# A decoder layer on eight cores: the last residual added by accumulating stores, norm stores moved to the GpSimd queue, and the first statistics interleaved with the K and V matmuls

## Chip, cores and metric

The kernel runs on one Trainium2 chip, as one program on all 8 cores (two dies of four). Each core computes 1024 of the 8192 tokens and reads all weights. The metric is the device time of the slowest core, in microseconds (us). Some executions of these kernels are in a second, slower state: the cores of one die show a lower granted TensorE clock and take longer (in one run of before, beside e1, cores 4 to 7 had a mean clock of 0.84 and took 7813 to 7819 us, cores 0 to 3 had 0.99 and took 6753 to 6769).

## The reference, cut

```python
# one layer, x is (1, 8192, 4096)
h = rms_norm(x, norm_mix_pre);  z = h @ w_in          # q, k, v, pool-in, two gates
y_attn = sliding_window_attention(q, k, v, sinks) @ w_branch_attn
y_pool = multiscale_pool(u, w_pool, pool_scale) @ w_branch_pool
merged = sigmoid(g_attn) * y_attn + sigmoid(g_pool) * y_pool
x = x + rms_norm(merged @ w_out, norm_mix_post)       # "x1": first residual norm
h = rms_norm(x, norm_ffn_pre)
up = causal_depthwise_conv(h @ w_up);  gate, val = split(up)
x = x + rms_norm((gelu(gate) * val) @ w_down, norm_ffn_post)      # "x2": second one
ple_gate = sigmoid(rms_norm(x, norm_ple_gate) @ w_ple_gate)
x = x + rms_norm(ple_gate * (p @ w_ple), norm_ple_post)           # last one, the output
```

A residual norm needs the sum of squares over all 4096 channels before it can scale the first of them. So its work comes in a burst, after the last matmul of one stage and beside the matmuls of the next.

## The kernel before

Features lie on partitions: D = 4096 is 32 chunks of 128, and a chunk of half the tokens is a 128x512 float32 tile of 256 KB. A scheduler records every operation of the program in order with its waits, and then each engine plays its own list. Every record comes from one helper, so all instructions carry one line number, L143 before and L144 after; they are told apart by their tiles.

Weights stream through a ring of 12 slots, each with a 256 KB slab of 8 blocks of 128x128. All weight loads are issued by GpSimd:

```python
def load_next(self):                       # cut
    i = self.nload % NS                    # NS = 12
    self.O("pool", "dma_start", [cast] if cast else [], [self.wringB[i]], dma=f"wr{i}",
           out=self.wring[i][:, 0:nk * 128], in_=src)

for kk in range(nk):                       # the matmuls of one slab, in run_jobs, cut
    self.O("pe", "matmul", [self.wringB[i]] + rb, [self.psB[bk]], ...)
    if side: ...self.side.popleft()()      # every `side` groups: one step of a norm
self.load_next()                           # then the load of the NEXT slab
```

In the program's order a load is only one slab ahead of the matmuls that use it. It runs farther ahead on the chip because GpSimd plays its list ahead of TensorE: a load waits only until TensorE has freed its slot (55 times and 95.1 us in the 130 us of before shown below), which allows up to 12 slabs, 96 groups of matmuls (a group is the matmuls with one 128x128 block).

The steps of a residual norm are put between the matmuls of the next stage by the `side` queue; each item taken from it is called a turn. Before, one step does everything for one chunk, and its store is on the Sync queue ("sp"):

```python
def main(k):                               # in norm_steps
    m, x, r = src[k], S["x"][k % NR], S["r"]
    O("dve", "tensor_tensor", [m.b, r.b], [m.b], out=m.v[:, 0:n], ..., op=ALU.mult)
    O("dve", "scalar_tensor_tensor", [m.b, x.b, constB], [m.b], ...)   # x gain, + residual
    ld_(k + NR)                            # residual chunk k+4, Sync queue
    put(k, m)                              # the store
    ...                                    # two ScalarE ops: square, and h in bf16
def put(k, m):                             # second norm
    O("sp", "dma_start", [m.b], [x2B[hf][k]], dma=f"x2s{k % 8}", out=x2_d[k][:, t0:t0 + 512], in_=m.v)
```

The last norm reloads x2 and adds it. Half 0 runs beside the matmuls of the per-layer-embedding stage (PLE, here also "last norm"); half 1 is the tail, after the last matmul:

```python
for f in range(NCH):                       # tail, cut
    m, x = R3[1][f], X2[f]                 # X2: x2 chunks loaded earlier
    O("dve", "tensor_tensor", [m.b, r.b], [m.b], out=m.v, in0=m.v, in1=r.v, op=ALU.mult)
    O("dve", "scalar_tensor_tensor", [m.b, x.b, constB], [m.b], ...)
    O("sp", "dma_start", [m.b], [outB], partial=True, dma="out", out=out_d[f][:, 512:1024], in_=m.v)
```

All those stores name one buffer, `outB`. The scheduler makes a writer wait for the buffer's earlier writers, with `partial=True` too:

```python
for b in writes:                           # Sched.op
    for d in (b.w, b.r):
        for k, v in d.items():
            if deps.get(k, 0) < v:
                deps[k] = v                # so each "out" store waits for the one before to land
```

The softmax here doesn't subtract the row's maximum and nothing guards it: scores larger than these inputs give would overflow.

## Time and profile before

| | before |
|---|---|
| times, us | 6766.01, 6785.48 (fast), 7415.28 (slow) |
| profiled span of the cores, us | 6735.2 to 6810.2 |
| TensorE idle, 0 to 560 us, core 6 | 93.7 |
| TensorE idle, 2200 to 3000 us (first norm), core 6 | 23.8 |
| TensorE idle, 5860 us to the last matmul (second norm and PLE), core 6 | 9.3 |
| last matmul to the end, core 6 | 78.3 |

The stage rows, here and later, are read from windows of 10 us: the part of each without TensorE busy, added up. "Lost to the clock" below is the busy time times one minus the granted clock of the window. I use core 6 for stages, because in the profiled execution of before cores 0 and 1 ran at a clock of 0.81 for much of the first 350 us (all of 200 to 340 us), and all four cores of their die at the end (0.81 from 6600 to 6680 us), while core 6's die was undisturbed (a mean clock of 0.990 to 0.991). Whole windows before that of the last matmul are counted, so up to 4 us of idle just before it are left out.

Lines of the page of the profile of before, slowest core (1): the span, busy time by engine, TensorE busy and its granted clock in 40 slices of the span in tenths, and the chain that ended last by engine.

```profile
span 6810.2 us, 104494 instructions; the slowest of 8 cores (6735.2 to 6810.2 us)
...
PE 6608.3 (97%) x41282; PEld 4044.9 (59%) x41282; DVE 1983.1 (29%) x2553; ACT 826.6 (12%) x1244; POOL 1335.0 (20%) x2501
...
PE   5999999999999998999999999999999999999995
...
PEclk7899999999999999999999999999999999999996
...
PE 92%; DMA 4%; DVE 2%; ACT 1%; issue 1%; POOL 0%; DVEq 0%; SPq 0%; ACTq 0%; POOLq 0%
```

TensorE is the bottleneck nearly everywhere: only the first and the last of the 40 slices, and a little the 16th (the first norm), are less than 90% busy. What a change elsewhere can win is therefore small, and what it can lose is not: TensorE has little idle time left in which a wait could hide (9.3 us on core 6 from 5860 us to the last matmul).

The chain that ended last, core 6 of before, from 0 to 200 us (start us, duration us, what):

```profile
22.04 47.36 DMA sb_arena<-w_in
...
73.61 17.50 DMA sb_arena<-xs
...
114.52 5.03 DMA sb_arena<-xs
...
144.46 5.70 DMA sb_arena<-xs
...
174.67 16.11 PE ps L143 x105
```

Each x slab holds up the chain again, since its statistics come after the K and V matmuls of the slab before. The streamed weights begin to be used near 175 us.

The waits of core 6 of before, 2580 to 2710 us, where the second half of the first norm runs (engine and tile, what it waited for, us in total, times, longest):

```profile
POOL sb_wr L143 <- PE ps L143: 95.1, 55, 5.9
...
DVE sb_arena L143 <- DMA sb_arena<-xr: 26.0, 14, 5.1
```

VectorE waits for the residual x, loaded by the Sync queue.

The tile `out` in the tail of core 6 of before (count, duration ns min/median/max, first and last start; then landing times):

```profile
L143 SPq DMA_DIRECT2D out<-sb_arena x32: 332/332/338, 6689.0 to 6760.1; - x32
...
DMA to landing us min/median/max: 2.0/2.1/2.7
```

32 stores take 71.1 us from first to last issue, (6760.1 - 6689.0)/31 = 2.29 us each, about the landing of one: this is the chain of stores through `outB`.

### The profile page before, as it was taken

What the parts mean: (1) busy time and instruction counts of PE and PEld (TensorE: products, weight loads), DVE (VectorE), ACT (ScalarE), POOL (GpSimd) and SP (SyncE); (2) the same over time, 40 slices, a digit from 0 to 9 for tenths busy, and PEclk for the clock granted to TensorE, in tenths of its full rate; (3) what the DMA queues carried; (4) which work ended last, traced back from release to release, by engine and by line L of the source; (5) the groups of instructions that cost most, each with busy time, mean ns of one, the idle gap of its engine ahead of it and who ended that gap; (6) DMA issues with size and microseconds to landing.
All of it is one profiled execution on the core that took longest, in us unless ns stands there. A gap on an engine that the chain in (4) does not pass through costs nothing.

```text
span 6810.2 us, 104494 instructions; the slowest of 8 cores (6735.2 to 6810.2 us)
## 1 busy us (share of the span) xinstructions
PE 6608.3 (97%) x41282; PEld 4044.9 (59%) x41282; DVE 1983.1 (29%) x2553; ACT 826.6 (12%) x1244; POOL 1335.0 (20%) x2501
## 2 busy tenths in 40 slices
PE   5999999999999998999999999999999999999995
PEld 3666666666665585766644566665456666444442
DVE  3343311111111125433300133331113333234343
ACT  2451000000001233000000000000000000023210
POOL 1011111111112322211111111111111111333331
PEclk7899999999999999999999999999999999999996
DMA  7457888888786577777799954446764444589683
GB/s 168 66 80 97 119 114 113 117 123 117 115 116 165 169 216 224 135 109 112 113 148 162 150 89 76 76 76 136 158 128 76 76 76 76 171 260 265 186 253 121
DMA packets 377375, 910.65 MB, mean 134 GB/s; under 512 B 50176, under 2 KB 72960, under 8 KB 371328
## 3 DMA queue, kind: packets, MB, share of 16 engines
q0 software_dynamic: 289344, 705.33, 60.3%
q1 hardware_dynamic: 87552, 198.64, 8.9%
q8 instruction: 337, 5.52, 0.3%
q14 instruction: 142, 1.16, 0.1%
HBM read 1297.47 MB, written 200.32 MB: 220 GB/s over the span
## 4 chain that ended last, share of the span: by engine, by line
PE 92%; DMA 4%; DVE 2%; ACT 1%; issue 1%; POOL 0%; DVEq 0%; SPq 0%; ACTq 0%; POOLq 0%
PE ps L143 92%; DVE sb_arena L143 2%; DMA out<-sb_arena 2%; DMA sb_arena<-xr 1%; ACT sb_arena L143 1%; DMA sb_arena<-w_in 1%; DMA sb_arena<-xs 0%; POOL sb_arena L143 0%; DMA sb_arena<-x_s 0%; DVEq L142 0%; ACT L143 0%; SPq L143 0%; ACTq L142 0%; SPq L142 0%; POOLq L168 0%
## 5 line engine op out<-in xcount | busy, mean ns | idle before, releaser
L143 PE MATMUL ps<-sb_arena,sb_wr 128*128 128x512 bf16 (+5 forms) x39744 | 6435.9, 324 | 20.1 <-DVE sb_arena L143 17.0
L143 PEld LDWEIGHTS ps<-sb_arena,sb_wr 128*128 128x128 bf16 x39744 | 3895.1, 98 | 2463.1 <-issue 112.6
L143 DVE TENSOR_TENSOR sb_arena<-ps,sb_arena 128x512 f32<-128x512 f32 (+9 forms) x892 | 682.2, 765 | 4011.9 <-PE ps L143 3800.9
L143 ACT ACTIVATE sb_arena<-sb_arena 128x512 f32<-128x512 f32 (+10 forms) x683 | 493.1, 725 | 4737.5 <-DVE sb_arena L143 4603.6
L143 POOL DMA_DIRECT2D sb_wr<-w_up x632 | 334.4, 529 | 1824.8 <-PE ps L143 1740.7
L143 DVE TENSOR_TENSOR sb_arena<-sb_arena 128x512 f32<-128x512 f32 (+8 forms) x543 | 450.7, 841 | 524.9 <-ACT sb_arena L143 496.0
L143 POOL DMA_DIRECT2D sb_wr<-w_in x384 | 204.6, 540 | 1333.1 <-PE ps L143 1333.1
L143 DVE SCALAR_TENSOR_TENSOR sb_arena<-sb_arena,sb_convp 128x1024 f32<-128x1024 f32 (+2 forms) x372 | 448.0, 1204 | 40.3 <-DVE sb_arena L143 1.8
L143 POOL DMA_DIRECT2D sb_wr<-w_down x256 | 135.5, 529 | 666.7 <-PE ps L143 645.3
L143 ACT ACTIVATE sb_arena<-ps 128x512 bf16<-128x512 f32 (+7 forms) x291 | 160.2, 550 | 779.7 <-PE ps L143 773.1
L143 PE MATMUL ps<-sb_arena 128*128 128x296 bf16 (+4 forms) x1216 | 199.0, 291 | 22.2 <-DVE sb_arena L143 12.0
L143 POOL DMA_DIRECT2D sb_wr<-b_out x256 | 137.4, 537 | 340.1 <-PE ps L143 318.3
L143 POOL DMA_DIRECT2D sb_wr<-b_down x256 | 137.4, 537 | 282.5 <-PE ps L143 248.5
L143 POOL DMA_DIRECT2D sb_wr<-b_pg x256 | 137.4, 537 | 261.7 <-PE ps L143 245.4
L143 PEld LDWEIGHTS ps<-sb_arena 128*128 128x128 bf16 (+1 forms) x1216 | 118.2, 105 | 105.2 <-issue 62.2
L143 DVE SCALAR_TENSOR_TENSOR sb_arena<-sb_arena,sb_gains 128x512 f32<-128x512 f32 (+1 forms) x192 | 144.7, 754 | 84.7 <-DMA sb_arena<-x_s 33.2
L143 PE MATMUL ps<-sb_arena,sb_ones_b 128*128 128x296 bf16 (+3 forms) x288 | 77.4, 353 | 80.5 <-ACT sb_arena L143 80.4
L143 DVE TENSOR_SCALAR sb_arena<-sb_arena,sb_convp 128x1024 f32<-128x1024 f32 (+2 forms) x186 | 143.7, 773 | 20.6 <-DVE sb_arena L143 0.5
L143 PEld LDWEIGHTS ps<-sb_arena,sb_ones_b 128*128 128x128 bf16 x288 | 27.4, 105 | 114.0 <-issue 97.8
L143 POOL DMA_DIRECT2D sb_wr<-b_up x112 | 60.6, 541 | 166.4 <-PE ps L143 156.8
L143 ACT ACTIVATE sb_arena<-sb_arena,sb_gains 128x512 bf16<-128x512 f32 (+1 forms) x128 | 90.7, 708 | 0.0
L143 POOL DMA_DIRECT2D sb_wr<-w_bp x64 | 33.8, 528 | 194.2 <-PE ps L143 190.7
(34 smaller groups left out, 392.7 us busy)
## 6 DMA issues: line engine op xcount, KB each, us to landing
sb_wr<-w_up POOLq DMA_DIRECT2D x632, 256.0 KB, 3.6
sb_wr<-w_in POOLq DMA_DIRECT2D x384, 256.0 KB, 5.1
sb_wr<-b_out POOLq DMA_DIRECT2D x256, 256.0 KB, 2.9
sb_wr<-b_pg POOLq DMA_DIRECT2D x256, 256.0 KB, 4.8
sb_wr<-w_down POOLq DMA_DIRECT2D x192, 256.0 KB, 5.6
sb_wr<-b_down POOLq DMA_DIRECT2D x192, 256.0 KB, 3.5
b_out<-w_out POOLq DMA_DIRECT2D x32, 1024.0 KB, 11.0
b_pg<-w_pg POOLq DMA_DIRECT2D x32, 1024.0 KB, 12.4
```

The lines of the kernel that those rows point to most:

```text
L143: inst = getattr(engine, fn[0])(**fn[1])
```

## The change

Its intent: shorten the start by loading the constants in two pieces on ScalarE's queue and putting the statistics of the next x slab between the K and V matmuls of this one; keep the residual loads from queueing behind stores by moving the x1 and x2 stores to GpSimd's queue, with the steps of a norm spread over several turns; and save the reload of x2 and one VectorE operation by storing x2 into the output and letting DMAs with `accum_op=ALU.add` add the last term to it. `RU` is the number of column blocks of `w_up` that are multiplied in two halves beside the first norm; with one turn per 13.5 groups instead of 12, 16 of them give room for the added turns. The core of the diff:

```diff
-RU = 14
+RU = 16
...
-        ld(gains...), ld(pscale...) ... 8 constant loads on "sp"
+        O("act", "dma_start", [], [constB], partial=True, dma="cst0", out=cf[:], in_=cf_d)
+        O("act", "dma_start", [], [constB], partial=True, dma="cst1", out=cb[:], in_=cb_d)
...
+            if s + 1 < NSL:
+                B.side.extend(stat_step(s + 1, q, hf) for q in range(4) for hf in range(2))
             for c in range(4):
...                                                     (K and V matmuls of slab s)
+                    if k % 15 == 14 and B.side:
+                        B.side.popleft()()
...
-            def step(k):                                (norm_steps)
+            def done(k):
+                put(k, src[k])
+                free(src[k])
+
+            def step(i):
                 def run():
-                    if k < NCH:
-                        main(k)
-                    if hout is not None and k >= 2:
-                        ss(k - 2)
+                    for lag, fn in ((0, scaled), (1, added), (2, done), (4, ss)):
+                        if 0 <= i - lag < NCH and (hout is not None or fn is not ss):
+                            fn(i - lag)
...
-                O("sp", "dma_start", [m.b], [x1B[hf][k]], dma=f"x1s{k % 8}", ...)
+                O("pool", "dma_start", [m.b], [x1B[hf][k]], dma=f"x1s{k % 8}", ...)
...
-                O("sp", "dma_start", [m.b], [x2B[hf][k]], dma=f"x2s{k % 8}", out=x2_d[k]...)
+                O("pool", "dma_start", [m.b], [x2B[hf][k]], dma=f"x2s{k % 8}", out=out_d[k]...)
...
-                O("sp", "dma_start", [m.b], [outB], partial=True, dma="out", out=out_d[k]..., in_=m.v)
+                O("pool", "dma_start", [m.b, x2B[hf][k]], [outB], partial=True, dma="out", out=out_d[k]...,
+                  in_=m.v, accum_op=ALU.add)
...                                                     (x2 reloads removed; the tail uses the same steps)
```

So `scaled(i)`, `added(i-1)`, the store `done(i-2)` and the sum of squares `ss(i-4)` now share a turn.

The listing of each engine's instructions with their waits shows GpSimd's list:

```
962 DMACopy sb_wr<-b_up 128x1024 [waits s_wr10,s_pe]
963 DMACopy x_s<-sb_arena 128x514 [waits s_dve,s_x1s4]
964 DMACopy sb_wr<-b_up 128x1024 [waits s_wr11,s_pe]
2502 DMACopy out<-sb_arena 128x512 [waits s_dve,s_out]
```

Between two weight loads there is now a store that waits for VectorE (`s_dve`), and in the PLE stage one that also waits for the landing of the store before it (`s_out`).

## The prediction

> What bounds the kernel. The page puts TensorE at 97% of the span; the chain of waits gives it 92%. Views by window show where it idles or slows:
> 1. Start, 0 to 182 us (K, V and first statistics): TensorE idle 70 to 80 us on every core. The constants load one after another on the Sync queue, so the first x load is issued at 14.2 us; statistics wait behind the previous slab's matmuls (waits of 17.9, 5.0 and 5.5 us for x in the chain).
> 2. Second half of the first norm, 2590 to 2700 us: idle 17 to 20 us on most cores (VectorE waits 21.8 us for the residual).
> 3. PLE stage, 6450 to 6600 us: VectorE waits 32.6 us for reloaded x2, TensorE idle about 12 to 20 us, then a clock of 0.81 to the end on the four cores of die 0.
> 4. Tail, after the last matmul (6737.8 us): 72 us. VectorE needs 1.53 us a step, 49 us, but the 32 stores are issued over 65.8 us, one per 2.06 us, and each lands in 2.0 us: in the code each waits for the landing of the one before, because all write the same output buffer.
>
> What the change does.
> Start: x loads leave at 1 us and are spread through the K/V matmuls. By my estimate from durations (x slab quarter about 5 us of DMA, K/V pass 21 us, weights landed by 70 us) the stage ends near 145 instead of 182 us: -37 us. Weight DMA still limits the first pass (DMA share 1.0 from 20 to 70 us).
> First norm: stores leave the Sync queue, squares and sums lag two more steps: -14 us. Second norm: -2 us.
> PLE: no x2 reload (16.8 MB), one VectorE operation fewer per step. But each accumulating store now sits in the GpSimd queue in order with the weight loads, and the listing of waits shows that it still waits for its predecessor to land. A step has 3.2 us; plain stores here took 4.5 us to land. I expect 4 us, so GpSimd falls behind by about 25 us against some 20 us of prefetched weights: small stalls. Net -10 us.
> Tail: VectorE needs only 0.75 us a step, but the chain is now 32 serial accumulating stores. A 256 KB GpSimd load lands in 2.7 us at best, a plain store in 2.0. [...] I estimate 3.2 us each, about 102 us plus 5: +36 us.
>
> Sum -27 us: 6750 us in the fast state (before: 6766 and 6785), range 6690 to 6800. Faster by over 2%: 0.05; within 2%: 0.90; slower: 0.05.
>
> What would show it. First matmul below 15 us, Q matmuls near 145 us instead of 186. Matmul idle near 2600 us under 6 us. No VectorE wait on x2. In the tail: 32 accumulating stores about 3.2 us apart, GpSimd waiting on their landing; VectorE done in about 25 us. Span from last matmul to end about 108 us.
>
> What would make it wrong. An accumulating store under 2.3 us makes the tail shorter than before (total near 6715). One over 4.5 us starves the weights in the PLE stage and lengthens the tail past 140 us (total over 6800). The 0.81 clock may vanish (-30 us) or spread. If weight DMA, not x, holds the first pass, the start gains only 15 us.

## The result

The changed kernel took 7127.96, 7122.84, 7170.85 and 7122.94 us, all fast; before took 6766.01 and 6785.48 (fast), 7415.28 and 7631.42 (slow) in the same rounds. The ratio of fast runs is 1.0532, 95% interval 1.0456 to 1.0608. A ratio here is the mean time of one kernel's fast runs over that of the other's of the same rounds, so it is not quite the ratio of the medians. The change made the kernel 5% slower, outside the predicted range.

Where the time went, core 6 (spans 6762.8 and 7126.4 us):

| stage | before: idle + lost to the clock, us | after, us | difference |
|---|---|---|---|
| start, 0 to 560 us | 93.7 + 14.3 | 69.4 + 10.3 | -28 |
| first norm, 2200 to 3000 us | 23.8 + 3.1 | 103.7 + 28.9 | +106 |
| second norm and PLE, 5860 us to the last matmul | 9.3 + 2.9 | 170.4 + 47.7 | +206 |
| last matmul to the end | 78.3 | 147.7 | +69 |

The sum is +353 of the 364 us between the spans. It closes less well than it looks: core 6's trace of after lacks 498 of its 41282 matmul records, and between 3000 and 5860 us this core shows 22.2 us of idle, where the six cores with all records show 4.3. The traces of e1 to e4 have the same gap on core 6, so its idle in these runs is some us too high. On core 7, complete in before and after, the four rows are -29, +89, +192 and +66 of 340 us. The third row of after is 110.5 + 35.7 us before 6600 us, the second norm, and 59.9 + 12.0 us after it, the last norm in the PLE stage: the second norm is the largest loss of all.

The same lines of the page of after, slowest core (6):

```profile
span 7126.4 us, 103902 instructions; the slowest of 8 cores (7096.8 to 7126.4 us)
...
PE 6606.3 (93%) x40784; PEld 4037.9 (57%) x41282; DVE 1933.8 (27%) x2500; ACT 827.7 (12%) x1245; POOL 1466.7 (21%) x2703
...
PE   7999999999999877999999999999999999877881
...
PEclk9999999999999998999999999999999999988995
...
PE 85%; DMA 8%; issue 3%; DVE 2%; ACT 1%; POOL 0%; DVEq 0%; POOLq 0%; ACTq 0%; SPq 0%
```

The busy time of TensorE looks the same, by chance: core 1 of before ran part of its work at 0.81, and core 6 of before has 6549.8 us. Holes have opened in slices 14 to 16 (the first norm) and in the last six (second norm, PLE, tail). The chain has lost 7 points of TensorE and gained 4 of DMA. GpSimd is 21% busy, hardly more than before, and the chain gives it 0%: by these shares it is no suspect. The 140.2 us that GpSimd waits in the first norm alone, with weight loads behind it (below), show in neither.

The chain at the start, core 6 of after:

```profile
78.51 20.30 DMA sb_arena<-xs
...
106.34 11.06 DMA sb_arena<-xs
...
147.53 14.63 PE ps L144 x105
```

The start won 174.67 - 147.53 = 27 us, and this part of the change works.

The waits of core 6 of after, 2560 to 2780 us, the second half of the first norm:

```profile
POOL x_s L144 <- DVE sb_arena L144: 140.2, 13, 21.8
DVE sb_arena L144 <- PE ps L144: 111.6, 16, 14.1
...
PE ps L144 <- DMA sb_wr<-b_up: 65.2, 14, 11.4
```

Read together, the three lines are a circle. GpSimd waits for VectorE, ahead of stores of x1, 13 times and 140.2 us in all. VectorE waits for TensorE. TensorE waits for weights. The wait for x in VectorE that was there before has gone: the intent was met, and it cost more than it gave.

One turn of the circle in the timeline of core 6 of after, GpSimd, VectorE and TensorE (start us, duration us, engine, operation, tiles, and in brackets the idle time before it and what ended that):

```profile
2620.06 0.54 POOL L144 DMA_DIRECT2D x_s<-sb_arena  x1 [5.49 <-DVE sb_arena L144]
...
2622.27 0.54 POOL L144 DMA_DIRECT2D sb_wr<-b_up  x1
...
2627.54 0.69 DVE L144 TENSOR_TENSOR sb_arena<-ps,sb_arena 128x512 f32<-128x512 f32 x1 [6.82 <-PE ps L144]
...
2631.12 0.75 DVE L144 SCALAR_TENSOR_TENSOR sb_arena<-sb_arena,sb_cf 128x522 f32<-128x522 f32 x1
...
2632.50 0.54 POOL L144 DMA_DIRECT2D x_s<-sb_arena  x1 [9.69 <-DVE sb_arena L144]
2633.04 0.54 POOL L144 DMA_DIRECT2D sb_wr<-b_up  x1
...
2639.84 0.58 PE L144 MATMUL ps<-sb_arena,sb_wr 128*128 128x512 bf16 x1 [8.51 <-DMA sb_wr<-b_up]
```

GpSimd issues a weight load at 2622.27 and then stands for 9.69 us at a store. VectorE cannot finish the chunk of that store, because ahead of its norm step lies an evacuation of `ps` (2627.54; it reads a finished sum of matmuls) that has waited 6.82 us for TensorE. When VectorE is done, at 2631.9 us, the store goes at 2632.50 and the next weight load at 2633.04; TensorE has been idle 8.51 us when its weights have landed at 2639.84.

So the store that wasn't ready held up more than itself: GpSimd issued nothing for the 9.69 us, and the weight load behind it in the list went only 0.54 us after the store.

The second half of the second norm, whose x2 stores now go into `out`: the waits of core 6 of after, 6310 to 6540 us.

```profile
POOL out L144 <- DVE sb_arena L144: 154.9, 15, 21.0
...
PE ps L144 <- DMA sb_wr<-b_pg: 49.0, 10, 7.9
```

It is the same circle. The PLE stage, second half, where the accumulating stores of half 0 run: the waits of core 6 of after, 6650 to 6850 us.

```profile
POOL out L144 <- DMA out<-sb_arena: 106.6, 31, 4.6
...
PE ps L144 <- DMA sb_wr<-b_pg: 39.8, 25, 5.1
```

Here GpSimd waits for the landing of the accumulating store before, 31 times, with the weights behind it. In before, VectorE waited there for x2; its stores waited for each other as well (97.0 us in the Sync queue's own waits between 6440 and 6600 us), but on the Sync queue, where nothing that TensorE needs stood behind them.

The tile `out` in the tail of core 6 of after, 6985 to 7130 us (the first of the 32 stores, at 6983.0 us, lies before this window):

```profile
L144 POOL DMA_DIRECT2D out<-sb_arena x31: 847/855/874, 6987.5 to 7121.8; - x31
...
  DMA out<-sb_arena: 101.5, 28
...
DMA to landing us min/median/max: 3.6/3.7/4.2
```

The stores follow at (7121.8 - 6987.5)/30 = 4.48 us, 0.85 us of issue and 3.7 us of landing. The prediction had 3.2, an estimate of its author.

A stall cost more than its length here. On core 6 of after, from 2570 to 2780 us in windows of 0.2 us, the granted clock is 0.50 in 11 stretches of 3.2 to 13.4 us, each of which begins while TensorE is idle. After the wait that ended at 2639.84 us it is 0.50 until 2644.2: the first four matmuls took 1.87 us, where at 1.00 thirteen took 2.97 (from 2645.30). Matmuls at a low clock make the 28.9 and 47.7 us lost in the table, over a quarter of the idle time that came with it.

### The profile page after: what moved, and what is told of

Read it like the earlier page. It is cut to its first block, busy times and chain, and to the rows that moved or that the text cites. A ratio compares the mean times of both kernels' runs of the same rounds, so it can differ in the third digit from the quotient of the medians.

```text
span 7126.4 us, 103902 instructions; the slowest of 8 cores (7096.8 to 7126.4 us)
## 1 busy us (share of the span) xinstructions
PE 6606.3 (93%) x40784; PEld 4037.9 (57%) x41282; DVE 1933.8 (27%) x2500; ACT 827.7 (12%) x1245; POOL 1466.7 (21%) x2703
## 3 DMA queue, kind: packets, MB, share of 16 engines
q0 software_dynamic: 308512, 759.87, 60.5%
## 4 chain that ended last, share of the span: by engine, by line
PE 85%; DMA 8%; issue 3%; DVE 2%; ACT 1%; POOL 0%; DVEq 0%; POOLq 0%; ACTq 0%; SPq 0%
PE ps L144 85%; DMA out<-sb_arena 4%; DVE sb_arena L144 2%; ACT sb_arena L144 1%; DMA sb_wr<-b_down 1%; DMA sb_wr<-b_up 1%; DMA sb_wr<-b_pg 1%; DMA sb_arena<-w_in 1%; DMA sb_wr<-b_out 1%; DMA sb_arena<-xs 0%; DMA sb_wr<-w_ple 0%; POOL sb_arena L144 0%; DVEq L143 0%; POOLq L143 0%; ACT L144 0%
## 5 line engine op out<-in xcount | busy, mean ns | idle before, releaser
L144 PE MATMUL ps<-sb_arena,sb_wr 128*128 128x512 bf16 (+6 forms) x39264 | 6447.9, 324 | 291.9 <-DMA sb_wr<-b_pg 88.8
L144 DVE TENSOR_TENSOR sb_arena<-ps,sb_arena 128x512 f32<-128x512 f32 (+10 forms) x896 | 683.1, 762 | 4300.7 <-PE ps L144 3620.4
L144 DVE SCALAR_TENSOR_TENSOR sb_arena<-sb_arena,sb_cf 128x1024 f32<-128x1024 f32 (+3 forms) x568 | 588.3, 1043 | 50.5 <-ACT sb_arena L144 10.2
L144 DVE TENSOR_TENSOR sb_arena<-sb_arena 128x512 f32<-128x512 f32 (+7 forms) x480 | 408.1, 861 | 567.4 <-ACT sb_arena L144 539.4
L144 POOL DMA_DIRECT2D out<-sb_arena x128 | 90.5, 707 | 560.7 <-DVE sb_arena L144 348.8
L144 DVE TENSOR_SCALAR sb_arena<-sb_arena,sb_cf 128x1024 f32<-128x1024 f32 (+3 forms) x316 | 182.5, 607 | 58.2 <-PE ps L144 24.1
L144 PE MATMUL ps<-sb_arena,sb_ones_b 128*128 128x296 bf16 (+3 forms) x270 | 70.6, 346 | 37.7 <-DVE ps L144 21.1
L144 ACT ACTIVATE sb_arena<-ps,sb_cf 64x386 f32<-64x386 f32 (+3 forms) x112 | 69.7, 623 | 261.4 <-PE ps L144 257.3
L144 POOL DMA_DIRECT2D x_s<-sb_arena x64 | 34.9, 545 | 271.8 <-DVE sb_arena L144 251.6
L144 ACT ACTIVATE sb_arena<-sb_arena,sb_cf 128x512 bf16<-128x512 f32 (+1 forms) x128 | 90.7, 708 | 0.0
```

Source lines behind the costliest of these rows:

```text
L144: inst = getattr(engine, fn[0])(**fn[1])
```

## Experiments

Three theories stood at the outset. **T1, queue order:** the stores in GpSimd's list wait for VectorE (or for the landing of the store before), and so destroy the run-ahead of the weight loads. **R1, contention:** the moved or accumulating stores take time of the DMA engines and of the queue that carries the weights, and weights land late. **R2, lagged steps:** the new order of VectorE's and ScalarE's work in the norms makes VectorE late, wherever the stores are. The tail was a question of its own: landing chain, accumulation, or DMA limit.

Every kernel gave the right result except e11. Its output is wrong, which doesn't matter for the time. The fast runs of before on the chips of these experiments were 6763 to 6823 us. "No ratio" below means that too few rounds had fast runs of both kernels.

| run | fast times, us | first norm, us | second norm and PLE, us | tail, us |
|---|---|---|---|---|
| before | 6766, 6785 | 23.8 + 3.1 | 9.3 + 2.9 | 78.3 |
| after | 7123, 7123, 7128, 7171 | 103.7 + 28.9 | 170.4 + 47.7 | 147.7 |
| e1 | 6856, 6861 | 21.9 + 0 | 55.0 + 11.7 | 146.2 |
| e2 | 7423 to 7439 | 242.7 + 60.5 | 309.9 + 82.1 | 82.1 |
| e3 | 6850, 6850, 6853 | 18.4 + 0 | 58.6 + 11.6 | 148.7 |
| e4 | 6744 to 6757 | 19.6 + 2.8 | 36.7 + 9.4 | 60.7 |
| e5 | 6707, 6709 | 2.5 + 0 | 11.6 + 3.0 | 61.1 |
| e6 | 6730, 6737, 6796 | 17.6 + 4.2 | 2.0 + 0 | 56.1 |
| e7 | 6700 | 15.4 + 0 | 7.0 + 2.8 | 55.7 |
| e8 | 6693, 6698, 6701 | 14.0 + 0 | 7.0 + 1.2 | 45.0 |
| e9 | 6740 | 17.9 + 4.0 | 13.6 + 4.5 | 84.2 |
| e10 | 6922, 6934 | 27.0 + 8.6 | 74.5 + 21.1 | 147.5 |
| e11 | 7033 (one run) | 92.7 + 27.8 | 133.9 + 37.3 | 97.7 |
| e12 | 6703, 6705 | 2.7 + 0 | 7.0 + 1.2 | 44.1 |

The stage columns are idle plus lost to the clock on core 6 of the profiled execution, as above. Differences of ten or twenty us in the first norm are within the spread between cores: among the eight cores of one execution its idle time goes from 4.7 to 25.3 us in before, from 2.5 to 18.0 in e5 and from 2.7 to 26.2 in e12.

### e1: the changed kernel with the x1 and x2 stores back on the Sync queue

```diff
-                O("pool", "dma_start", [m.b], [x1B[hf][k]], ...
+                O("sp", "dma_start", [m.b], [x1B[hf][k]], ...
-                O("pool", "dma_start", [m.b], [x2B[hf][k]], ...
+                O("sp", "dma_start", [m.b], [x2B[hf][k]], ...
```

> The changed kernel with only the x1 and x2 stores of the norm steps moved back from the GpSimd queue to the Sync queue; lagged steps and accumulating output stores stay. Theory T1 (a store in the GpSimd queue waits for VectorE's current step, so the weight loads behind it lose their run-ahead of up to 12 slabs and TensorE runs dry): the four norm stages, which now lose about 250 us of idle and low clock together (counted on core 7), lose under 30 us, and the time is about 6890 us (6850 to 6930). Rival R1 (the stores take DMA time or ring room from the weight loads, whoever issues them): at most half is won, over 6990 us. Rival R2 (the longer lag between the parts of a step stalls TensorE): no change, over 7080 us.

Measured: 6856 and 6861 us fast (7380 and 7517 slow; no ratio). The stalls of the first and second norm are gone (21.9 us of idle in the first), while those of the PLE stage and the tail, which hang on the accumulating stores, are nearly as in after (58.8 us of idle and low clock in the PLE stage, 71.9 in after; the second norm has 7.8 instead of 146.2). The lagged steps are still in this kernel, so R2 falls. T1 asks for this, and R1 does too if what is contended for is the queue that the weights share; e3 has to tell them apart.

### e2: the kernel before with its x1 and x2 stores on GpSimd's queue

```diff
-                O("sp", "dma_start", [m.b], [x1B[hf][k]], ...
+                O("pool", "dma_start", [m.b], [x1B[hf][k]], ...
-                O("sp", "dma_start", [m.b], [x2B[hf][k]], ...
+                O("pool", "dma_start", [m.b], [x2B[hf][k]], ...
```

> The kernel before with only the x1 and x2 stores moved to the GpSimd queue: the reverse of the first run. T1: TensorE waits for weights in the four norm stages as in the changed kernel, the store following its VectorE step even closer, so 7000 to 7100 us. R1: some of it, 6850 to 6950. R2: no change, about 6780 us.

Measured: 7423 to 7439 us, all fast, ratio 1.0926 (1.0897 to 1.0954). That is more than I had expected. Two words changed in the kernel before make it 9% slower. Here the store stands right behind its VectorE operation in the program (a lag of 0), so by T1 no group of matmuls is left as run-ahead. The waits of core 6 of e2, 2690 to 2970 us:

```profile
POOL x_s L143 <- DVE sb_arena L143: 210.5, 17, 23.3
...
PE ps L143 <- DMA sb_wr<-b_up: 126.3, 14, 13.1
```

They are the lines of after, only longer.

### e3: the changed kernel with the stores of the norms placed eight turns later

```diff
-                    for lag, fn in ((0, scaled), (1, added), (2, done), (4, ss)):
+                    for lag, fn in ((0, scaled), (1, added), (DL, done), (4, ss)):
```

`DL` is 10 for the two norms with a residual and stays 2 for the last one; the number of turns is lengthened to match.

> The changed kernel with the x1 and x2 stores still on the GpSimd queue, but issued 10 steps after their step began instead of 2, so that VectorE is done when GpSimd, running up to 12 slabs (96 matmul groups, 7 to 8 steps) ahead of TensorE, comes to them. Same stores, same queue, same bytes. T1: the stalls of the four norm stages go, about 6890 us (6850 to 6940), like the first run. R1 (bytes or ring room of the stores): stalls stay, over 7050 us. R2: stays over 7050 us.

This is the run that tells T1 from R1. The same stores are on the same queue, with the same bytes; only their place in the list is later, so VectorE has long finished a chunk when GpSimd comes to its store. Measured: 6850, 6850 and 6853 us fast (7647 slow), ratio 1.0077 (1.0048 to 1.0106), as good as taking the stores off the queue (e1). The waits of core 6 of e3, 2540 to 2680 us:

```profile
POOL sb_wr L144 <- PE ps L144: 54.7, 44, 2.9
...
PE ps L144 <- DMA sb_wr<-b_up: 12.2, 12, 2.2
```

GpSimd waits for ring slots again, as before the change. Now the DMA issues of the weights in that window, with the median time to landing last, for after and then for e3:

```profile
sb_wr<-b_up POOLq DMA_DIRECT2D x69, 256.0 KB, 6.1
```

```profile
sb_wr<-b_up POOLq DMA_DIRECT2D x68, 256.0 KB, 13.3
```

And the busy share of the DMA engines over the same windows in 40 slices, in tenths, for after (5.5 us a slice) and then for e3 (3.5 us a slice):

```profile
DMA  0331903945581595098309803902935574190897
```

```profile
DMA  7799999999999999999998999999999999556555
```

In e3 a weight takes twice as long to land as in after, the DMA engines are busier, and TensorE doesn't stall; in after they stand idle again and again while TensorE waits for weights. R1 falls for these two stages: the weights were not slow, they were asked for late.

### e10: a lag of 3

> The changed kernel with the x1 and x2 stores on GpSimd issued 3 steps after the step began (2 in the change, 10 in the third run). T1 in numbers: at the store the weight loads can be ahead of TensorE by the matmuls between VectorE's part and the store, one step (13.5 matmul groups, 3 us) with lag 2, two steps (6 us) with lag 3; a weight load takes 5 to 6 us to land. So lag 3 should remove most of the stalls, about 6900 us (6860 to 6960), against 7125 with lag 2 and 6851 with lag 10. If the lag mattered only by moving stores apart from the loads of x, there would be little difference between 2 and 3: over 7050.

The edit is that of e3 with `DL = 3`. Measured: 6922 and 6934 us fast (7188 slow), ratio 1.0211 (1.009 to 1.0331). The time follows the lag of the store: 0 in e2 about 7430 us, 2 in after 7125, 3 here 6928, 10 in e3 6851. (e2 is otherwise the kernel before, without the accumulating stores and the new start, so its place in the row is only rough.) A single turn more is worth about 200 us, since what counts is how many matmuls lie between VectorE's operation and the store: one turn with a lag of 2, two with 3.

### e4: e1, and the accumulating stores no longer chained by their landings

```diff
-        outB = Buf("out")
+        outB = [[Buf(f"out{p}_{c}") for c in range(NCH)] for p in range(2)]
-                O("pool", ..., [m.b, x2B[hf][k]], [outB], partial=True, dma="out", ...
+                O("pool", ..., [m.b, x2B[hf][k]], [outB[hf][k]], dma=f"out{k % 8}", ...
```

> The first run plus: each accumulating output store writes its own buffer record and one of 8 semaphores, so it no longer waits for the landing of the store before. The tail after the last matmul (133 us in the changed kernel, 32 stores 4.47 us apart: 0.85 us issue and 3.7 us to landing) falls to 40 to 50 us if only the chain of landings made it long, limited by 32 issues of 0.85 us; if the DMA engines need 4.4 us for an accumulating store, the tail stays near 133 us. In the PLE stage the stores still wait for VectorE in the GpSimd queue, so some stalls stay there. About 6790 us (6750 to 6830); over 6870 if the chain is not the cause of the long tail.

Measured: 6744 to 6757 us, four fast runs, ratio 0.9931 (0.9906 to 0.9956). The chain through one buffer was worth about 105 us against e1, most of it in the tail (146.2 to 60.7 us on core 6). I had expected a tail of 40 to 50 us. The tile `out` of core 6 of e4 shows why it stopped short:

```profile
L144 POOL DMA_DIRECT2D out<-sb_arena x32: 847/855/2086, 6684.4 to 6730.1; - x32
...
DMA to landing us min/median/max: 5.4/10.8/17.1
```

Stores now leave every (6730.1 - 6684.4)/31 = 1.5 us and land after 10.8. The windows view of 6690 to 6700 us (us, busy time of PE, PEld, DVE, ACT and POOL, clock, DMA share, GB/s), for before and then for e4, with 6720 to 6730 us of e4 as well:

```profile
6690.00:6700.00 10.00, 0.00 (x0) 0.00 (x0) 8.96 (x14) 0.00 (x0) 0.00 (x0) 0.50 0.33 124
```

```profile
6690.00:6700.00 10.00, 0.00 (x0) 0.00 (x0) 10.00 (x16) 0.00 (x0) 5.68 (x7) 0.50 1.11 153
...
6720.00:6730.00 10.00, 0.00 (x0) 0.00 (x0) 0.00 (x0) 0.00 (x0) 6.80 (x8) 0.50 1.12 201
```

The DMA engines show a share above 1 at 153 GB/s of accumulating stores, where plain stores gave 124 GB/s at a third of their time. By share, I estimate that a plain store would reach 124/0.33 = 376 GB/s and the accumulating one 153/1.11 = 138: 2.7 times the engine time per byte. At the measured 153 GB/s, 256 KB take about 1.7 us. But the last line gives 201/1.12 = 179 GB/s, 2.1 times. The other cores of the same trace show when: core 5 had 180 and 181 from 6670 to 6690 us and 134 in the next 10 us, where core 4, whose stores begin at 6684.1 us, stored too; core 6 had 138 to 150 from 6690 to 6720 us and 179 after that, when core 7 was nearly done (its span ends at 6723.8 us; each core's time is counted from its own start). So in this trace the accumulating stores of a core took more engine time per byte (2.7 times that of plain stores) while the neighbour core stored too than while it hardly did (2.1). That the neighbour is the cause is not shown: no experiment isolates it.

### e5: e4, with the stores of the last norm placed eight turns later

> The fourth run (Sync stores, no chain of landings) plus: in the last norm the accumulating stores are issued 10 steps after their step began instead of 2, so that GpSimd no longer waits for VectorE with weight loads behind. If what remains of the PLE stage's stalls (25 us idle and 8 us of low clock in the fourth run) is again the run-ahead of the weight loads, they fall under 10 us and the time is about 6725 us. If the DMA engines are the limit (an accumulating store takes them about 1.7 us, one comes each 3.2 us, the weights take about half of their time), the stalls stay near 25 us and the time stays at 6745 to 6755.

The edit is the `DL` of e3, with 10 for the last norm and 2 for the others. In e4 the PLE stage still lost time (36.7 + 9.4 us with the second norm), and two causes were left: stores waiting for VectorE at a lag of 2, or the DMA engines, which the accumulating stores load more (2.1 to 2.7 times the time per byte, by the shares in e4). Measured: 6707 and 6709 us fast (7004, 7494 and 7553 slow), ratio 0.9884 (0.9842 to 0.9927), the idle time 11.6 us (over all eight cores the stages fall from a mean of 41.5 us of idle and low clock in e4 to 11.3). The total is lower than the 6725 I expected; this chip also ran before some 17 us faster than that of e4 (6773 to 6789 us against 6792 and 6806). The bytes are the same, so the DMA engines weren't the limit in that stage; it was the order of the queue again. In the tail their share is still 1.09 to 1.15 (core 6, 6640 to 6680 us; the tail is 61.1 us).

### e11: the changed kernel without `accum_op`

```diff
-                  in_=m.v, accum_op=ALU.add)
+                  in_=m.v)
```

> Wrong result on purpose: the changed kernel with the accumulating taken out of the output stores, which then overwrite out; queue, chain and order are the same. It measures what accumulating costs by itself: 0.85 us of issue and 3.7 us to landing with it. Without it I expect 0.54 us and 2.7 us, a store each 3.3 us, a tail of about 110 us instead of 133. If the GpSimd queue and the chain alone make the 4.47 us, the tail stays at 133.

The result lacks x2 (relative error 0.865), as meant. This measures a plain GpSimd store in the same chain. The tile `out` in the tail of core 6 of e11:

```profile
L144 POOL DMA_DIRECT2D out<-sb_arena x32: 539/539/548, 6925.2 to 7015.6; - x32
...
DMA to landing us min/median/max: 2.2/2.3/2.7
```

A plain store takes 0.54 us to issue and 2.3 to land, and they follow at (7015.6 - 6925.2)/31 = 2.92 us; the accumulating ones took 0.85, 3.7 and 4.48. So of the +69 us of the tail, about 32 x (4.48 - 2.92) = 50 us are the accumulation and about 32 x (2.92 - 2.29) = 20 us the move of the chain from Sync to GpSimd. (My expectation speaks of a tail of 133 us in after; that was a misreading, from the last matmul it is 147.7.) The stalls of the two norms stay: 92.7 + 27.8 us in the first, and 112.8 + 32.8 of the 133.9 + 37.3 in the second. They have nothing to do with accumulation. Those of the PLE stage fall from 59.9 + 12.0 us to 21.1 + 4.5: that fits a plain store each 2.92 us, faster than the prediction's step of 3.2 us, and an accumulating one each 4.48 us, slower than it.

### e6: the kernel before without the chain of its output stores

> The kernel before with one thing changed: its output stores on the Sync queue no longer wait for the landing of the store before. If that chain set the pace of its tail (a store each 2.06 us against a VectorE step of 1.53 us) and held up the reload of x2 behind it on the Sync queue in the PLE stage, the tail falls from 72 to about 55 us and the PLE stalls from 12 to 20 us to under 5: about 6750 us in the fast state against 6785. If the DMA engines set the pace, nothing changes.

The edit is that of e4, made in the kernel before, where the stores are plain and on Sync. Measured: 6730, 6737 and 6796 us counted as fast (8050 slow), ratio 0.9952 (0.9826 to 1.0078). The tail shortens from 78.3 to 56.1 us, and the second norm and PLE from 9.3 + 2.9 to 2.0 + 0. In the profile cores 6 and 7 ran at a clock of 0.81 at the start, which cost 90 us on core 6 there, and cores 4 and 5 from 6380 us on, so the total is unclear; the tail, in which no matmul runs, is not.

### e9: the kernel before with the new start alone

> The kernel before with only the start of the change: constants in two loads on the ScalarE queue, x loads first on the Sync queue, statistics of the next slab between the K and V matmuls. In the changed kernel's trace the first matmul with streamed weights starts at 147.5 us instead of 186.2. Fast state: 38 us less than before, about 6740 us; if something later gives it back, 6765 or more.

Measured: 6740 us in the one fast run (6879, 6931, 7474 and 7567 slow; before 6763, 6769 and 6823 fast on the same chip; no ratio). The streamed weights are in use at 146.1 us instead of 175.6, and the span of core 6 falls from 6762.8 to 6738.0 us: 25 us, from one execution of each. (The 186.2 of the expectation is core 1, at its low clock.)

### e7 and e8: what is left when the costs are taken out

e7 is the changed kernel with all stores back on Sync, x2 reloaded from the output, plain stores without the chain. e8 is e7 with 15 of the 32 chunks of the tail done by accumulating GpSimd stores, so that VectorE has one operation less for these and two queues share the tail.

```diff
+            for f in range(NCH):                       (tail of e8)
+                if f in ACC:                           # 0, 2, ... 28; empty in e7
+                    O("dve", "scalar_tensor_tensor", [m.b, r.b, constB], [m.b], ...)       # no residual
+                    O("pool", "dma_start", [m.b], [x2B[1][f]], dma=f"oa{f % 8}", ..., accum_op=ALU.add)
+                    continue
```

> The changed kernel with Sync stores, and with the last residual reloaded from out and added on VectorE, stored by plain Sync stores without a chain; no accumulating store is left. The start and the lagged steps stay. Tail about 55 us (32 VectorE steps of 1.53 us), PLE stalls under 10 us: about 6715 us. If accumulating is better than reloading, it is slower than the late accumulating run; if reloading is better, faster.

> The reload version, but in the tail 15 of the 32 chunks are added by accumulating stores on GpSimd (one VectorE operation of 0.75 us, about 1.7 us of DMA) and 17 by VectorE with reloaded x2 (1.53 us, plain store). VectorE needs about 38 us and the DMA engines about 37 us at the same time, so the tail should be 43 to 48 us, 8 to 12 us less than the reload version: about 6705 us. If the two kinds of store disturb each other, no gain.

Measured: e7 6700 us in its one fast run (6816, 6833 and 7537 slow; no ratio), tail 55.7 us. e8: 6693, 6698 and 6701 us fast (7440 slow), ratio 0.9868 (0.984 to 0.9897), tail 45.0 us. e8 has the shortest tail but e12's, and is 1.3% faster than before and 6% faster than the change; its total can't be told apart from e7's single fast run. In the tail, accumulation is useful: no weight loads stand behind it there, and with 15 accumulated chunks of 32 the DMA engines moved 222 to 228 GB/s of both kinds of store at a share of 1.09 to 1.12 (core 6 of e8, 6650 to 6680 us), where e4, with 32, had 151 to 167 from 6690 to 6720 us.

### e12: e8 without the lagged steps

```diff
-                    for lag, fn in ((0, scaled), (1, added), (2, done), (4, ss)):
+                    for lag, fn in ((0, scaled), (0, added), (0, done), (2, ss)):
```

> The best version so far (eighth run: Sync stores, no chain, half of the tail accumulated, 6693 to 6701 us fast) with the lags of the norm steps taken back to those of the kernel before (store and squares right behind their VectorE operation, sums two steps later). If the lagged steps are worth what was predicted (14 us in the second half of the first norm), about 6712 us; if the waits there come from the DMA load of x, under 6703.

Measured: 6703 and 6705 us fast (7706 and 7714 slow; no ratio), against 6693 to 6701 of e8 on another chip. With the stores on Sync, the lagging is worth some 7 us by these times, which runs on two chips can't separate from nothing: the mean idle and low clock of the first norm over the eight cores is 17.1 us in e12, 16.2 in e8 and 11.4 in e7. It also shows that a lag of 0 does no harm when the store is on the Sync queue; in e2, on GpSimd's, it cost 9%.

## Why the prediction was wrong

**The failed step** is the one on what a store in GpSimd's queue costs. For the first norm the prediction said "stores leave the Sync queue, squares and sums lag two more steps: -14 us" and for the second -2 us, and only for the accumulating stores did it see the weights behind: "GpSimd falls behind by about 25 us against some 20 us of prefetched weights: small stalls". It took the 20 us of prefetched weights as given. But the run-ahead is not a property of the ring; it exists only because GpSimd waits for nothing but ring slots. A store in its list that waits for VectorE ties GpSimd to VectorE (140.2 us of waits in the second half of the first norm of after), VectorE is tied to TensorE through the evacuations in front of it (111.6 us), and TensorE to the weights behind the store (65.2 us). The run-ahead shrinks from 96 groups of matmuls to the groups between VectorE's operation and the store. The runs showed +106 us in the first norm and +206 in the second norm and PLE stage. The same move alone makes the kernel before 9% slower (e2), undoing it removes the norm stalls (e1), and keeping it with a later place in the queue removes them as well (e3), with weights that land more slowly (13.3 us against 6.1). Queue order is therefore shown, and contention refuted, for the norms.

Point by point:

- *Start, -37 us.* The mechanism was right, the size was off: 28 us on core 6, about 25 us alone (e9). The 37 was read from core 1, which ran at a clock of 0.81 there; on core 1 the first streamed matmul did move by 38 us, from 186.2 to 148.4, but part of that is the low clock gone.
- *First norm, -14 us.* Wrong in sign: +106 us. What was to be gained was small as well: with the stores on Sync, e1 has 21.9 us of idle where before has 23.8 + 3.1.
- *Second norm, -2, and PLE, -10 us.* Wrong in sign: +206 us together, of which +146 are the second norm and +60 the PLE stage. In the PLE stage the prediction named the wait for the landing, with the weights behind it, but judged it nearly harmless. Moving the x2 stores to Sync (e1), taking the chain away (e4) and placing the accumulating stores later in the list (e5) brought these stages from 170.4 + 47.7 us to 55.0 + 11.7, to 36.7 + 9.4 and to 11.6 + 3.0.
- *Tail, +36 us.* The mechanism was right, 32 serial accumulating stores, and the term was mis-sized: 4.48 us a store instead of 3.2, hence +69 us instead of +36. The 3.2 was the author's estimate, set above the landings of 2.0 and 2.7 us that it quotes; the kernel before, the only one it had seen run, has no accumulating store. Of the missing 1.28 us, issue is a part: 0.85 us, where a plain GpSimd store takes 0.54; the landing takes 3.7 us where a plain one takes 2.3 (e11).
- *What would make it wrong.* It named an accumulating store over 4.5 us that starves the PLE stage. The store was at that limit, 4.48, but the larger losses came in the two norms, which have no accumulating store.

What stays open: what the neighbour core does to an accumulating store (e4), and why after was fast in all four runs while before was often slow. No run tested these.

## What to carry to other kernels

Before an operation that waits for a compute engine is put into the queue that prefetches weights, ask how many matmuls lie in the program between the event it waits for and its own place: in this kernel that number, not the depth of the ring, was the run-ahead that was left (after with a lag of 2 turns 7125 us, of 3 6928, of 10 6851). Put such a store on another queue, or so late in the list that its wait has always been met (here eight turns later, 7125 to 6851 us). Look also for chains of landings that one shared output buffer creates: the stores here go to different bytes, and the results were right without the chain (e4, e6). Cutting it was worth about 20 us in the tail of before (e6; its total is unclear) and about 105 us in e4 against e1.
